# Where the large buffers and weight tiles begin in a partition: a two-layer hybrid trunk on one core

## The chip, the cores and the metric

One core of a Trainium2 chip. The metric is the device time of one launch in microseconds (us). The kernel before takes 2214.97 us, the median of three runs (2214.35 to 2215.24).

## The reference

The input is 256 tokens of 2048 float32 channels. Layer 0 is a hybrid mixer: an RMSNorm, one input projection (2048 to 11296 columns), a Mamba-2 state-space group of 32 heads and a stick-breaking attention group of 16 heads, and one output projection from the 4096 joined channels. Layer 1 is a pooling mixer with trailing means of 2, 4, 8 and 16 tokens and a linear map of 512 by 512 for each of its four groups. Each layer ends in an MLP with a squared ReLU. In the reference's words:

```python
def sq_relu_mlp(h, w_up, w_down):
    u = jax.nn.relu(h @ w_up)
    return (u * u) @ w_down

for layer in range(DEPTH):
    ...
    x = x + mix.astype(x.dtype)
    x = x + sq_relu_mlp(rms_norm(x, mlp_norm[layer]), mlp_w_up[layer], mlp_w_down[layer]).astype(x.dtype)
```

With a hidden width of 8192 the two MLPs hold most of the multiplications; every weight is read from HBM once.

## The kernel before

All products with weights form one stream. `plan()` lists it as units (a block of output columns) and steps (what one DMA of 512 KB brings: two k-tiles of 512 columns, or four of 256). For each step SP loads the weights into a `raw` tile, ScalarE copies them to a `hi` tile (line 182) and VectorE puts the rest into a `lo` tile (line 183); `feed` keeps loads six steps and splits three steps ahead of TensorE. The activations lie in the same form, a high and a low part, in fourteen large buffers that `slot(i)` hands out (`st0` to `st13`, 8192 bytes in each partition: high or low part, four k-tiles, 256 tokens). A product is made of three: high by high, low by high, high by low, all in the type float32r. Small work (norms, the state-space scan, attention, pooling) is cut into generators that `tick` advances between steps, so that its TensorE instructions stand between those of the stream.

There are two orders of a product, and in each TensorE reads two things from SBUF: the moving operand that it streams now, and the stationary weights of the next product, which it loads meanwhile.

- Not turned (line 820: the projections to B, z, q, k, v, the output projection, `down`, `pool`): the activations in `st` are stationary, 128 by 128; the weights in `hi` or `lo` move, 512 columns (256 in the last two units, 288 in one). Three products for each k-tile and half of the tokens.
- Turned (lines 812 and 814: `c1`, the eight `x` units and all `up` units): 128 columns of `hi` or `lo` are stationary ("weights that stay"), and the activations in `st` move: line 812 streams both parts of a k-tile (2 by 256 columns) against `hi`, line 814 the high part (256 columns) against `lo`. One of each is a pair here; a unit has 32 pairs.

**Where tiles begin.** A tile pool gives each tag its place in a partition when the tag is first used, one behind the other, each rounded up to 32 bytes. Before the pool lie a scratch area of 16384 bytes for dynamic DMAs and 128 bytes of constants. The first places are `cst` (2560 bytes), `prm` (808), `row` (384), `mhalf` (32) and three `ev` tiles; then the large tags follow in the order in which the stream first needs them, with small ones between. So the built kernel before has these starting addresses modulo 256 (in bytes, the same in each partition):

| tiles | start modulo 256 | what they hold |
|---|---|---|
| `hi`, `lo` (4 of each, 4096 bytes) | 96 | split weights |
| `st0`, `st1`, `st2`, `st3` | 96 | normed input of layer 0's projection and `up`; hidden of layer 1's blocks 0, 2 |
| `st8`, `st9` | 96 | merged heads; hidden of layer 0's blocks 1, 3; normed input of layer 1's `up` |
| `st10`, `st11` | 192 | the same as `st8`, `st9` |
| `st4`, `st7` | 128 | merged heads; hidden of layer 0's blocks 0, 2 and of layer 1's blocks 1, 3 |
| `st5`, `st6` | 64 | the same as `st4`, `st7` |

Within these tiles every operand begins a multiple of 512 bytes from the start (of 128 in the one unit of 288 columns). Below, the **distance** of a product is the start of the weights loaded during it minus the start of what it streams, modulo 256.

The MLPs run as blocks: eight `up` units (256 turned pairs), then four `down` units (384 products of 512 columns), four such blocks for each layer. Where the hidden values of a block lie is set by `gen_u`'s `base`, `((4, 8), (0, 4))[layer][b % 2]`.

Of the kernel before, what the change touches and what calls it, by code (L numbers as in the profile page):

```python
# [11 lines left out]
F32R = mybir.dt.float32r  # L12
# [4 lines left out]
P = 128  # L17
# [7 lines left out]
NB = DFF // FB  # L25
WINS = (2, 4, 8, 16)

# columns of the input projection: z | x | B | C | dt | q | k | v
CZ, CX, CB, CC = 0, 2048, 4096, 4608
CQ, CK, CV = 5152, 7200, 9248  # L30

# per-partition parameters (channel = tile * 128 + partition)
P_HYB, P_MLP, P_POOL, P_CW, P_CB, P_ON, P_QN, P_KN = 0, 16, 48, 64, 160, 184, 200, 201
NPRM = 202

# constant matrices
K_ID, K_U, K_SL, K_ONE, K_LT = 0, 128, 256, 384, 512
NCST = 640

# where in the weight stream (unit, k-tile) the quarters of x for the first norm are loaded  # L40
X_EARLY = ((0, 14), (1, 2), (1, 6), (1, 10))
AHEAD_LOAD = 6
WARM = 2
AHEAD_SPLIT = 3


def plan():
    """The products with weights in their order. A unit is a block of output columns; a step is
    the part of its weights that one DMA brings: [128, k-tiles, columns]."""
    units = []  # L50

    def unit(w, r0, nk, c0, n, kind, arg, src, k0=0, turned=False):
        units.append(dict(w=w, r0=r0, nk=nk, c0=c0, n=n, kind=kind, arg=arg, src=src, k0=k0,
                          turned=turned))

    unit("w_in", 0, KT, CB, 512, "b", None, "h")
    unit("w_in", 0, KT, CC + 256, 288, "c2", None, "h")
    unit("w_in", 0, KT, CC, 256, "c1", None, "h", turned=True)
    for g in range(4):
        for h in range(2):  # L60
            unit("w_in", 0, KT, CX + 512 * g + 256 * h, 256, "x", (g, h), "h", turned=True)
        unit("w_in", 0, KT, CZ + 512 * g, 512, "z", g, "h")
    for j in range(4):
        unit("w_in", 0, KT, CK + 512 * j, 512, "k", j, "h")
        unit("w_in", 0, KT, CQ + 512 * j, 512, "q", j, "h")
        unit("w_in", 0, KT, CV + 512 * j, 512, "v", j, "h")
    for c in range(4):
        unit("w_out", 0, 2 * KT, 512 * c, 512, "out", c, "merged")
    for layer in range(2):
        if layer == 1:  # L70
            for g in range(4):
                unit("pool_w", 512 * g, 4, 0, 512, "pool", g, "pool", 4 * g)
        for b in range(NB):
            for i in range(8):
                unit("w_up", D * layer, KT, b * FB + 256 * i, 256, "up", (layer, b, i),
                     f"mlp{layer}", turned=True)
            for c in range(4):
                n = 256 if (layer, b, c) == (1, NB - 1, 3) else 512
                for c0 in range(512 * c, 512 * c + 512, n):
                    unit("w_down", DFF * layer + b * FB, KT, c0, n, "down", (layer, b, c), "u")  # L80

    steps, off = [], 0
    for u, d in enumerate(units):
        ks = list(range(0, d["nk"], 4 if d["turned"] else 2))
        if u == 0:
            ks = [0, 1, 2, 3] + ks[2:]
        for k, e in zip(ks, ks[1:] + [d["nk"]]):
            steps.append((u, k, e - k, off))
            off += (e - k) * P * d["n"]
    return units, steps  # L90
# [3 lines left out]
def tile_trunk(ctx: ExitStack, tc: tile.TileContext, x_in, xt_in, w_all, prm_in,  # L94
# [27 lines left out]
    def v3(ap, a, b):  # L122
        return ap.rearrange("p (a b) -> p a b", a=a, b=b)

    # ------------------------------------------------------------ constants
    x_sb = []
    cst = new("cst", [P, NCST])
    prm = new("prm", [P, NPRM])
# [7 lines left out]
        return prm[:, i : i + 1]  # L136

    def load_x(q):
        """half of the tokens' rows, half of the columns at a time"""
        m, c = q // 2, slice(D // 2 * (q % 2), D // 2 * (q % 2) + D // 2)  # L140
        if q == 0:
            x_sb[:] = [slot(12 + m, (P, D), F32) for m in range(MT)]
        nc.sync.dma_start(x_sb[m][:, c], x_in[m * P : m * P + P, c])

    # ------------------------------------------------------------ the weight stream
    hT, merged = {}, {}
    u_blk, pT, hM = {}, {}, [{}, {}]
    sources = {"h": hT, "merged": merged, "pool": pT, "mlp0": hM[0], "mlp1": hM[1], "u": u_blk}
# [21 lines left out]
    def split(i):  # L170
        u, k, nk, _ = steps[i]
        n = units[u]["n"]
        raw = raws.pop(i)
        if u == 0:
            for kk in range(k, k + nk):
                if kk % 4 == 0:
                    hx.append(slot(kk // 4))
                put_hi_lo(hx[-1], kk % 4, xt[kk // 8][:, kk % 8], pcol(P_HYB + kk))
                hT[kk] = (hx[-1], kk % 4)
        hi, lo = (v3(new(tag, [P, 1024], F32R, bufs=4)[:, : nk * n], nk, n)  # L180
                  for tag in ("hi", "lo"))
        act.activation(hi, raw, AF.Copy)  # L182
        dve.tensor_tensor(lo, raw, hi.bitcast(F32), ALU.subtract)  # L183
        splits[i] = hi, lo
# [6 lines left out]
            split(done["split"])  # L191
            done["split"] += 1

    # ------------------------------------------------------------ work beside the weight stream
    lane, lane2 = deque(), deque()
    flags = set()

# [14 lines left out]
            assert lane or lane2  # L212
            tick()

    # ------------------------------------------------------------ norms
    def power(dst, src, mean):
        """dst = (src * mean + eps) ** -0.5"""
        n = src.shape[-1]
        t = new("pw", [P, 8], bufs=2)[:, :n]
        dve.tensor_scalar(t, src, mean, EPS, ALU.mult, ALU.add)  # L220
        pool.tensor_tensor(dst, t, mhalf[:, :n], ALU.pow)  # L221

    def put_hi_lo(dst, c, ps, gain=None):
        """dst[:, 0/1, c] = the high and low parts of ps (times a per-partition gain)"""
        if gain is None:
            act.activation(dst[:, 0, c], ps, AF.Copy)  # L226
            dve.tensor_tensor(dst[:, 1, c], ps, dst[:, 0, c].bitcast(F32), ALU.subtract)  # L227
        else:
            act.activation(dst[:, 0, c], ps, AF.Copy, scale=gain)  # L229
            dve.scalar_tensor_tensor(dst[:, 1, c], ps, gain, dst[:, 0, c].bitcast(F32),  # L230
                                     ALU.mult, ALU.subtract)

    def to_ring(src, tiles, kt0, dst, gain):
        """src[m]: [128 tokens, 512]; four k-tiles of 256 tokens into dst and tiles[kt0...]"""
        for h in range(2):
            b = bank()
            bv = v3(b, 2, T)
            for c in range(2):
                for m in range(MT):
                    k = 2 * h + c  # L240
                    pe.transpose(bv[:, c, m * P : (m + 1) * P],  # L241
                                 src(m)[:, k * P : (k + 1) * P], ident)
            if gain is None:
                put_hi_lo(dst, slice(2 * h, 2 * h + 2), bv)
            else:
                for c in range(2):
                    put_hi_lo(dst, 2 * h + c, bv[:, c], pcol(gain + kt0 + 2 * h + c))
            for c in range(2):
                k = 2 * h + c
                tiles[kt0 + k] = (dst, k)  # L250
            yield
# [1 line left out]
    rs = {}  # L253

    def spread(name):
        """rs[name, "row"][p, t] = rs[name] of token t, for all p"""
        r = rs[name]
        dg = v3(t4(2 * P), MT, P)
        for m in range(MT):
# [7 lines left out]
        rs[name, "row"] = o  # L267

    def add_halves(dst, ps):
        """dst = the sum of the two halves of each bank"""  # L270
        act.activation(dst, ps[:, :, T:], AF.Copy)  # L271
        dve.tensor_tensor(dst, ps[:, :, :T], dst, ALU.add)  # L272

# [21 lines left out]
        if c == 3 and name != "pool":  # L295
            yield from spread(name)

    # ------------------------------------------------------------ SSD
    ssd = {}

    def evac(ps, n, r):
# [3 lines left out]
        return e  # L305

    def turn(e, n):
        """e: [tokens, n * 128 channels] -> [channel, n, 3 + 256 tokens]"""
        yield
        yield  # L310
        xT = v3(t4(n * 259), n, 259)
# [14 lines left out]
        return xT  # L326

    def conv(xT, ct0, n, dst):
        """xT: [channel, n, 3 + 256 tokens] -> dst [channel, n, 256 tokens] = silu(conv + b)"""
        dve.memset(xT[:, :, 0:3], 0.0)  # L330
        for c in range(n):
            w = P_CW + 4 * (ct0 + c)
# [7 lines left out]
                yield  # L340

    def gen_dt(pre):
        """pre: [128, 64] dt before softplus, (chunk, head)"""
        e, t, q, da = (ssd["tmp"][:, 1792 + 64 * i : 1856 + 64 * i] for i in range(4))
        # log1p(e) = 2 artanh(e / (2 + e)), e = exp(-|pre|) in (0, 1]
        act.activation(e, pre, AF.Abs)
        act.activation(e, e, AF.Exp, scale=-1.0)
        dve.tensor_scalar(t, e, 2.0, None, ALU.add)
# [153 lines left out]
        dst = slot(8 + g)  # L502
        yield from to_ring(lambda m: y[:, m], merged, 4 * g, dst, P_ON)

    # ------------------------------------------------------------ stick-breaking attention
    at = {}

    def gen_qk(kind, j, e):
# [113 lines left out]
                merged[16 + 4 * j + 2 * i + h] = (dst, 2 * i + h)  # L622
            yield

    # ------------------------------------------------------------ MLP and pooling
    def gen_u(i, ea, eb, base):
        yield
        act.activation(eb, ea, AF.Square)  # L628
# [117 lines left out]
            dve.scalar_tensor_tensor(ea, ea, 0.0, row2(name), ALU.max, ALU.mult)  # L746
            lane.append(gen_u(i, ea, eb, ((4, 8), (0, 4))[layer][b % 2]))

    # ------------------------------------------------------------ the stream
    act.dma_start(prm, prm_in)  # L750
    act.preload_act_table_set("silu_and_others")
    mhalf = new("mhalf", [P, 8])
    pool.memset(mhalf, -0.5)
    # keeps the tensor engine's clock up until the first weights are there
    wt = new("ev", [P, MT, 512], bufs=3)
    dve.memset(wt[:, 0], 0.0)
    wb = bank()
# [3 lines left out]
    hx, late = [], []  # L761

    def startup():
        """the first norm's scale and small constants"""
        ss = new("ss", [P, MT, 4], bufs=2)
        for q in range(4):
            m, h = q // 2, q % 2
# [20 lines left out]
    i = 0  # L788
# [103 lines left out]
```

## Time and profile before

| | |
|---|---|
| median of three runs | 2214.97 us |
| span of the profiled execution | 2214.3 us |
| TensorE busy | 2207.0 us in 11045 instructions |
| weight loads beside it | 1854.0 us |
| VectorE, ScalarE, GpSimd busy | 1325.4, 1113.0, 21.7 us |
| read from HBM | 412.57 MB, 187 GB/s over the span |

The page gives no time for the profiled execution beyond its span; the span lies 0.7 us under the median. "Busy" of TensorE counts a modelled end, and the spans of neighbours overlap, so the mean duration of a matmul (389 ns) is longer than the time from one start to the next. Where TensorE never idles, that time (the pitch) is the busy time of a window divided by the products in it; a window's count also holds one to three products that reach over its edges, so the products are counted here from the code.

### The profile page before, as it was taken

The numbers are of one execution on the slowest core, as the hardware profiler recorded it, in microseconds if no ns is written. First come the engines' busy times: TensorE is split into PE (matmuls) and PEld (weight loads), VectorE is DVE, ScalarE is ACT, GpSimd is POOL, SyncE is SP. The second block draws the span as 40 slices with busy tenths as digits, with TensorE's granted clock in tenths as the row PEclk, the third lists the DMA queues.
The fourth block names the chain that finished last, engine by engine and source line by source line (L and its number), as shares of the span: only waits on it lengthen the run. The fifth ranks groups of instructions, "written<-read, shape, count | busy, mean of one in ns | idle before, by whom it ended". The sixth has DMA issues, their size and how long they took to land.

```text
span 2214.3 us, 28392 instructions
## 1 busy us (share of the span) xinstructions
PE 2207.0 (100%) x11045; PEld 1854.0 (84%) x11045; DVE 1325.4 (60%) x1554; ACT 1113.0 (50%) x1325; POOL 21.7 (1%) x21
## 2 busy tenths in 40 slices
PE   9999999999999999999999999999999999999999
PEld 7888888888888888888888888888888888888888
DVE  6988756655645565555555466577555645655654
ACT  7665456665544454354344345456534534544543
POOL 0000000000000000000000000000000000000000
PEclk9999999999999999999999999999999999999999
DMA  8654555555665566556566666555666656565564
GB/s 300 213 196 162 163 184 167 163 179 170 202 187 184 181 186 186 189 186 189 187 189 190 204 219 190 181 171 163 190 196 187 188 189 190 187 193 191 190 195 148
DMA packets 118630, 416.56 MB, mean 188 GB/s; under 512 B 13344, under 2 KB 16096, under 8 KB 118240
## 3 DMA queue, kind: packets, MB, share of 16 engines
q1 hardware_dynamic: 117632, 413.60, 59.0%
q8 instruction: 86, 1.41, 0.3%
q10 hardware_dynamic: 864, 1.15, 0.2%
q14 instruction: 48, 0.39, 0.1%
HBM read 412.57 MB, written 2.13 MB: 187 GB/s over the span
## 4 chain that ended last, share of the span: by engine, by line
PE 99%; DMA 0%; DVE 0%; ACT 0%; issue 0%; SPq 0%; DVEq 0%; ACTq 0%
PE acc L820 58%; PE acc L812 25%; PE acc L814 13%; PE bg L469 1%; PE bg L241 1%; DMA raw<-w_all 0%; PE bg L526 0%; PE bg L616 0%; PE bg L561 0%; PE bg L437 0%; PE bg L557 0%; PE bg L618 0%; PE bg L474 0%; PE bg L480 0%; DVE lo L183 0%; PE bg L577 0%
## 5 line engine op out<-in xcount | busy, mean ns | idle before, releaser
L183 DVE TENSOR_TENSOR lo<-raw,hi 128x1024 fp32r<-128x1024 f32 (+2 forms) x774 | 931.4, 1205 | 777.5 <-ACT hi L182 762.9
L182 ACT ACTIVATE hi<-raw 128x1024 fp32r<-128x1024 f32 (+2 forms) x774 | 808.5, 1045 | 1033.8 <-PE acc L820 642.7
L820 PE MATMUL acc<-hi,st 128*128 128x512 f32 (+2 forms) x3840 | 1175.2, 389 | 1.4 <-ACT hi L182 1.4
L820 PEld LDWEIGHTS acc<-hi,st 128*128 128x128 f32 x3840 | 709.9, 188 | 153.4 <-ACT hi L182 3.5
L812 PE MATMUL acc<-st,hi 128*128 128x512 f32 x2336 | 826.1, 398 | 0.0
L820 PE MATMUL acc<-lo,st 128*128 128x512 f32 (+2 forms) x1920 | 740.7, 387 | 0.1
L814 PE MATMUL acc<-st,lo 128*128 128x256 f32 x2336 | 654.8, 280 | 0.0
L812 PEld LDWEIGHTS acc<-st,hi 128*128 128x128 f32 x2336 | 438.3, 188 | 106.1 <-issue 1.4
L814 PEld LDWEIGHTS acc<-st,lo 128*128 128x128 f32 x2336 | 440.5, 189 | 2.0 <-issue 1.2
L820 PEld LDWEIGHTS acc<-lo,st 128*128 128x128 f32 x1920 | 360.4, 188 | 78.1 <-DVE lo L183 0.5
L706 DVE TENSOR_TENSOR st<-st,acc 128x512 f32<-128x512 f32 (+1 forms) x74 | 46.5, 669 | 29.1 <-PE acc L820 29.1
L746 DVE SCALAR_TENSOR_TENSOR ev<-ev,rrow 128x512 f32<-128x512 f32 x64 | 44.3, 692 | 2.2
L227 DVE TENSOR_TENSOR st<-ev,st 128x512 fp32r<-128x512 f32 x64 | 44.3, 692 | 0.2
L272 DVE TENSOR_TENSOR ev<-acc,ev 128x512 f32<-128x512 f32 x64 | 43.7, 683 | 0.0
L226 ACT ACTIVATE st<-ev 128x512 fp32r<-128x512 f32 x64 | 40.6, 634 | 2.0
L229 ACT ACTIVATE st<-bg,prm 128x256 fp32r<-128x256 f32 x64 | 28.4, 468 | 24.9 <-DVE st L230 22.8
L628 ACT ACTIVATE ev<-ev 128x512 f32<-128x512 f32 x64 | 39.5, 617 | 0.0
L271 ACT ACTIVATE ev<-acc 128x512 f32<-128x512 f32 x64 | 37.2, 582 | 0.0
L230 DVE SCALAR_TENSOR_TENSOR st<-bg,prm,st 128x256 fp32r<-128x256 f32 x64 | 29.4, 478 | 6.0 <-ACT st L229 6.0
L336 DVE SCALAR_TENSOR_TENSOR t<-t,prm,t 128x256 f32<-128x256 f32 x48 | 19.6, 476 | 0.0
L221 POOL TENSOR_TENSOR qrs<-pw,mhalf 128x8 f32<-128x8 f32 x8 | 15.6, 1952 | 246.4 <-DVE pw L220 246.4
L516 DVE TENSOR_TENSOR ev<-ev,qrs 128x1024 f32<-128x1024 f32 x8 | 9.8, 1225 | 13.5 <-POOL qrs L221 13.5
(155 smaller groups left out, 595.7 us busy)
## 6 DMA issues: line engine op xcount, KB each, us to landing
raw<-w_all SPq DMA_DIRECT2D x746, 512.0 KB, 3.5
raw<-w_all SPq DMA_DIRECT2D x20, 256.0 KB, 3.1
st<-x_in SPq DMA_DIRECT2D x8, 512.0 KB, 5.3
st<-scr SPq DMA_DIRECT2D x8, 512.0 KB, 5.8
raw<-w_all SPq DMA_DIRECT2D x8, 288.0 KB, 4.5
st<-prow_in SPq DMA_DIRECT2D x2, 1024.0 KB, 5.3
st<-xt_in SPq DMA_DIRECT2D x6, 256.0 KB, 6.3
st<-pmat_in SPq DMA_DIRECT2D x1, 768.0 KB, 5.1
```

The source lines that it names most:

```text
L182: act.activation(hi, raw, AF.Copy)
L183: dve.tensor_tensor(lo, raw, hi.bitcast(F32), ALU.subtract)
L226: act.activation(dst[:, 0, c], ps, AF.Copy)
L227: dve.tensor_tensor(dst[:, 1, c], ps, dst[:, 0, c].bitcast(F32), ALU.subtract)
L271: act.activation(dst, ps[:, :, T:], AF.Copy)
L272: dve.tensor_tensor(dst, ps[:, :, :T], dst, ALU.add)
L628: act.activation(eb, ea, AF.Square)
L706: dve.tensor_tensor(x_sb[m][:, cs], x_sb[m][:, cs], ps[:, m, : d["n"]], ALU.add)
L746: dve.scalar_tensor_tensor(ea, ea, 0.0, row2(name), ALU.max, ALU.mult)
L812: pe.matmul(ps[:, f].rearrange("p (h t) -> p h t", h=2), hi[:, kk, fs], t[:, :, c], start=first, stop=False)
L814: pe.matmul(ps[:, f, :T], lo[:, kk, fs], t[:, 0, c], start=False, stop=last)
L820: pe.matmul(ps[:, m, :n], t[:, h % 2, c, m * P : (m + 1) * P], (hi, hi, lo)[h][:, kk], start=first and h == 0, stop=last and h == 2)
```

## The change

The constants of the module get `PAD, TURN = 24, 56`. Ahead of all other tiles the kernel takes a tile `pad` of 24 floats, then one tile of each of the fourteen `slot`s, then four tiles each of `hi` and `lo`, none of which is used; this fixes the places of these tags. `hi` and `lo` grow from 1024 to 1088 floats, 4352 bytes, which is 17 times 256. A turned unit uses its tile from float 56 on, which is 224 bytes; all others from float 0. The scratch area for dynamic DMAs shrinks from 16384 to 1024 bytes. Comments go. No instruction is added, removed or moved.

```diff
+PAD, TURN = 24, 56
 ...
+    new("pad", [P, PAD])
+    for i in range(14):
+        slot(i)
+    for tag in ("hi", "lo"):
+        for _ in range(4):
+            new(tag, [P, 1088], F32R, bufs=4)
 ...
-        hi, lo = (v3(new(tag, [P, 1024], F32R, bufs=4)[:, : nk * n], nk, n)
+        o = TURN if units[u]["turned"] else 0
+        hi, lo = (v3(new(tag, [P, 1088], F32R, bufs=4)[:, o : o + nk * n], nk, n)
                   for tag in ("hi", "lo"))
 ...
-    nc = _bacc.Bacc("TRN2", target_bir_lowering=False, num_devices=1)
+    nc = _bacc.Bacc("TRN2", target_bir_lowering=False, num_devices=1,
+                    dynamic_dma_scratch_size=1024)
```

## The prediction

> **What bounds the kernel now.** I read the page's busy times first, then the chain that ended last, then the busy time by stage, then TensorE's timeline inside a stage. The page:
>
> ```profile
> span 2214.3 us, 28392 instructions
> PE 2207.0 (100%) x11045; PEld 1854.0 (84%) x11045; DVE 1325.4 (60%) x1554; ACT 1113.0 (50%) x1325; POOL 21.7 (1%) x21
> ...
> PEclk9999999999999999999999999999999999999999
> ...
> PE acc L820 58%; PE acc L812 25%; PE acc L814 13%; PE bg L469 1%; PE bg L241 1%; DMA raw<-w_all 0%; PE bg L526 0%; PE bg L616 0%; PE bg L561 0%; PE bg L437 0%; PE bg L557 0%; PE bg L618 0%; PE bg L474 0%; PE bg L480 0%; DVE lo L183 0%; PE bg L577 0%
> ```
>
> TensorE is never without work (2207.0 of 2214.3 us), its granted clock is full in all slices, and 96% of the chain is lines 820, 812 and 814. So the time is a number of products times the pitch from one start to the next, and only a change of the pitch counts. The feed is ahead, as the view of waits shows: ScalarE's split waits for TensorE to free a `hi` tile, while TensorE's weight loads waited for a split for 3.5 us in the whole span.
>
> ```profile
> engine line waited for: us in total, times, longest us
> ...
> ACT hi L182 <- PE acc L820: 642.7, 414, 4.1
> ...
> PEld acc L820 <- ACT hi L182: 3.5, 4, 1.3
> ```
>
> Now the view of busy time by stretch, for stretches that begin and end with whole units or runs of k-tiles (us, then busy time and count of TensorE, weight loads, VectorE, ScalarE, GpSimd, then clock and DMA):
>
> ```profile
> core 0: us, PE busy (x) PEld busy (x) DVE busy (x) ACT busy (x) POOL busy (x), PEclk, DMA share, GB/s
> 834.17:923.74 89.57, 89.57 (x387) 72.05 (x385) 44.80 (x41) 35.64 (x36) 0.00 (x0) 1.00 0.60 188
> 1587.93:1675.01 87.08, 87.08 (x387) 72.07 (x385) 44.80 (x41) 35.71 (x36) 0.00 (x0) 1.00 0.62 193
> 1014.18:1102.71 88.53, 88.53 (x386) 72.19 (x385) 44.79 (x41) 35.75 (x36) 0.00 (x0) 1.00 0.62 190
> 1193.16:1282.74 89.58, 89.58 (x386) 72.05 (x385) 46.88 (x45) 35.62 (x36) 0.00 (x0) 1.00 0.66 213
> 1373.19:1464.52 91.33, 91.33 (x411) 74.53 (x409) 53.49 (x59) 44.68 (x59) 0.00 (x0) 1.00 0.58 184
> 1764.65:1854.22 89.57, 89.57 (x386) 72.05 (x385) 44.80 (x41) 35.62 (x36) 0.00 (x0) 1.00 0.60 188
> 2120.59:2187.77 67.18, 67.18 (x291) 54.04 (x289) 32.19 (x31) 25.87 (x28) 0.00 (x0) 1.00 0.59 181
> 2187.77:2210.33 22.56, 22.56 (x193) 22.52 (x191) 10.86 (x17) 8.20 (x13) 0.00 (x0) 1.00 0.48 149
> 2142.98:2148.58 5.60, 5.60 (x26) 4.51 (x24) 3.65 (x4) 2.09 (x2) 0.00 (x0) 1.00 0.85 259
> 2148.58:2159.78 11.20, 11.20 (x49) 9.00 (x48) 4.90 (x4) 4.27 (x5) 0.00 (x0) 1.00 0.61 198
> 2190.61:2196.21 5.60, 5.60 (x50) 5.60 (x49) 2.75 (x5) 2.54 (x4) 0.00 (x0) 1.00 0.71 210
> ```
>
> The first two are the key: both are four `down` units of 384 equal products (line 820, 512 columns), with the same DMA load and other work. In the first the hidden values lie in `st4` to `st7` (distances 32 and 224, from the table of places) and a product takes 89.57 / 384 = 233.3 ns; in the second they lie in `st0` to `st3` (distance 0), 87.08 / 384 = 226.8 ns. The third, half at 0 and half at 96, stands between: 230.5. Within one unit at distances 32 and 224, the ninth row has 24 products at 32 (233.3 ns each) and the tenth 48 at 224 (233.3). So a distance of 0 is worth 6.5 ns of each such product. The eleventh row is 48 products of 256 columns at 224: 116.7 ns.
>
> **The part that I can read off: products that are not turned.** By the same rule of places the kernel after starts its pool at 1024 + 128 = 1152; `pad` takes 96 bytes, so `st0` begins at 1248, which is 224 modulo 256. All fourteen `st` are 8192 bytes and all `hi` and `lo` 4352, both multiples of 256: all begin at 224. So every product of line 820 gets distance 0, and 226.8 ns (in the unit of 288 columns the k-tiles alternate between 0 and 128, as now: nothing). By stretch, against 87.08:
>
> - layer 0's `down`: blocks 0 and 2, 89.57 and 89.58: -2.49 and -2.50; blocks 1 and 3, half of them off distance: -1.45 each (the second, 91.33, also holds norms, which stay);
> - layer 1's `down`: block 1, 89.57: -2.49; block 3, the 288 products of 512 columns: 67.18 against 288 x 0.2268 = 65.3, -1.9; its last 192 products of 256 columns (22.56 us, 117.5 ns each) have no row at distance 0; half of a product of 512 at distance 0 would be 113.4 ns, so the gain lies between 0 and -0.8, and I take -0.3;
> - the output projection: 24 of its 32 k-tiles lie off distance (`st4` to `st7`, `st10`, `st11`), so 4 x 144 products x 6.5 ns: -3.7;
> - q, k, v, z, B and `pool` are at 0 already: nothing.
>
> Sum: -16.3 us.
>
> **The part that I can't: turned pairs.** Here the activations move from 224 and the weights are loaded from 224 + 224 = 448, 192 modulo 256: distance 224 for all 2336 pairs (c1 and x 9 units, `up` 64, 32 pairs each). Now they stand at 0, or, for half of layer 1, at 160 (`st10`, `st11`). Two stretches of eight `up` units, layer 0 and layer 1, and the halves of one of layer 1's units:
>
> ```profile
> 923.74:1014.18 90.44, 90.44 (x513) 78.41 (x512) 54.02 (x55) 45.37 (x53) 0.00 (x0) 1.00 0.59 187
> 1675.01:1764.65 89.64, 89.64 (x514) 78.41 (x512) 54.02 (x55) 45.40 (x53) 0.00 (x0) 1.00 0.61 188
> 1531.93:1537.49 5.56, 5.56 (x35) 4.90 (x34) 4.12 (x5) 3.76 (x5) 0.00 (x0) 1.00 0.60 189
> 1537.49:1543.13 5.64, 5.64 (x35) 4.90 (x33) 2.73 (x3) 2.12 (x2) 0.00 (x0) 1.00 0.68 189
> ```
>
> A pair takes 353.3 ns in layer 0 (90.44 / 256) and 350.2 in layer 1; in the halves 347.5 (distance 0) and 352.5 (160). So distance 0 alone does not fix a pair: layer 0 and that first half have the same distance. The timeline shows two steady patterns (start, then duration):
>
> ```profile
> 924.08 0.40 PE L812 MATMUL acc<-st,hi 128*128 128x512 f32 x1
> 924.32 0.28 PE L814 MATMUL acc<-st,lo 128*128 128x256 f32 x1
> 924.43 0.40 PE L812 MATMUL acc<-st,hi 128*128 128x512 f32 x1
> 924.67 0.28 PE L814 MATMUL acc<-st,lo 128*128 128x256 f32 x1
> 924.79 0.40 PE L812 MATMUL acc<-st,hi 128*128 128x512 f32 x1
> 925.03 0.28 PE L814 MATMUL acc<-st,lo 128*128 128x256 f32 x1
> 925.14 0.40 PE L812 MATMUL acc<-st,hi 128*128 128x512 f32 x1
> ...
> 1533.67 0.39 PE L812 MATMUL acc<-st,hi 128*128 128x512 f32 x1
> ...
> 1534.71 0.39 PE L812 MATMUL acc<-st,hi 128*128 128x512 f32 x1
> ```
>
> In layer 0 three unequal pairs repeat: 0.35, 0.36, 0.35, together 1.06 us, 353.3 each. In layer 1 three pairs take 1534.71 - 1533.67 = 1.04 us, 346.7 each. No pair stands at 224 in this trace. The bounds: from below 226.8 + 113.4 = 340.2, the best product of 512 and half of it; from above the slowest pair of the three, 924.43 to 924.79, about 361. The nearest rows are those at 224 in line 820: 233.3 + 116.7 = 350.0. Against them speaks that all steady pairs fall into a few patterns, the best at 346.7. I take the middle of the two, 348.3. Per 256 pairs that is 89.17:
>
> - layer 0's `up`: 90.44 to 89.17, -1.27, four times: -5.1;
> - layer 1's `up`: 89.64 to 89.17, -0.47, four times: -1.9;
> - c1 and x, 288 pairs among other work that hides which pattern they have: between 346.7 and 353.3, so 0 within 1 us.
>
> Sum: -7.0 us. With the bounds: at 340.2, -13.4 - 10.2 - 2.9 = -26.5; at 361, +7.9 + 11.1 + 3.2 = +22.2.
>
> **What costs nothing.** The unused tiles issue nothing, and no order on any queue changes. The DMAs are as many, and land in `raw` at another place; a load of 512 KB lands in 3.5 us, and six are ahead:
>
> ```profile
> raw<-w_all SPq DMA_DIRECT2D x746, 512.0 KB, 3.5
> ```
>
> If that cover went, a step of line 820 (12 products, 2.7 us) would have to wait for a load; TensorE would gain gaps. The scratch area serves a queue that this kernel doesn't use for data: weights come by SP's. About 610 other products (transposes, scan, attention) get new places too; at some ns each, 2 us either way.
>
> **Sum.** 2214.97 - 16.3 - 7.0 = 2191.7 us. The profiled execution (2214.3) is 0.7 us under the median, so its terms carry over.
>
> **Rivals.**
>
> - *Nothing happens: 2215 us.* The difference between the two `down` stretches would come from something that goes with the buffers, not with their start. For it: distance and buffer change together in all rows. Against it: the stretch on `st8` to `st11`, of which half begin like `hi`, stands halfway (230.5 ns). The Trainium skill ("SBUF — State Buffer", section "SBUF: two separate sides") says that TensorE has two independent read ports for the moving operand and the weights and never waits on anyone; by that rule where the operands begin would not matter, and this rival would be the outcome. The rows (233.3 against 226.8 ns) disagree with it. Chance 0.06.
> - *The turned pairs gain nothing:* 224 keeps them between 350.5 and 354, as 160 does (352.5). That is -2.4 to +5.8 us instead of -7.0: 2196 to 2204 us. For it: line 820 is slower at 224 than at 0. Chance 0.22.
> - *The turned pairs fall to a pattern that this trace doesn't have,* 340 to 345 ns: 2172 to 2183 us. For it: the best products of line 820 and half of one add up to that; against it, no steady pattern of the trace is that fast. Chance 0.16.
> - *The turned pairs get slower:* weights loaded 32 bytes behind the stream collide with it in lines 812 and 814, and the streams of line 814, half as long, are stalled as often. At 361 ns everywhere the time is 2214.97 - 16.3 + 22.2 = 2220.9. It is slower than before from 16.3 / 2336 = 7.0 ns above today's mean of about 351.5, at 358.5. For it: the slow third pair is a collision of this kind. Chance 0.06, half of it on the slow side.
>
> **How the numbers follow.** My forecast (pairs at 345 to 350.5) has 0.50 and its own range is 2183 to 2196. From 2174 to 2205 about 0.82 lies: below stay the deepest cases of the third rival, above the first and last. A measurement here tells 0.2% (4.4 us) from no change. Faster: 0.50 + 0.22 + 0.16 = 0.88; the first rival and the milder half of the last give 0.08 for the same, and 0.04 is slower.
>
> **What would show it.** Stretches of four `down` units at 87.1 us in both layers, whatever block; a stretch of the output projection about 0.94 us shorter for each unit; eight `up` units near 89.2, the same in layer 0 and layer 1, with one steady pattern. Unchanged DMA rows and waits of TensorE. Wrong it would be if `down` at distance 0 kept 89.57 in blocks 0 and 2 (then the start is not the cause), or if `up` stretches passed 91.8 (358.5 ns).

## The result and the profile after

The changed kernel takes 2189.57 us (median of four runs, 2188.69 to 2189.96), against 2215.10 us for the kernel before beside it: a ratio of 0.9884, 95% interval 0.987 to 0.9898. The forecast was 2191.7 us, 2174 to 2205.

First the page, then the view of busy time by stretch (start and end in us, then length, and busy time and count of TensorE, weight loads, VectorE, ScalarE, GpSimd, the clock and DMA), for the stretches that answer to those shown of before. Lines 812, 814 and 820 of before are 823, 825 and 831 here.

```profile
span 2187.9 us, 28392 instructions
...
PE 2180.8 (100%) x11045; PEld 1857.1 (85%) x11045; DVE 1325.4 (61%) x1554; ACT 1115.1 (51%) x1325; POOL 21.7 (1%) x21
```

```profile
core 0: us, PE busy (x) PEld busy (x) DVE busy (x) ACT busy (x) POOL busy (x), PEclk, DMA share, GB/s
555.20:737.94 182.74, 182.74 (x825) 151.42 (x823) 98.35 (x102) 87.53 (x106) 0.00 (x0) 1.00 0.62 195
828.29:915.35 87.06, 87.06 (x387) 72.08 (x386) 44.77 (x41) 35.84 (x36) 0.00 (x0) 1.00 0.62 193
915.35:1004.10 88.75, 88.75 (x514) 78.67 (x513) 54.05 (x55) 45.41 (x53) 0.00 (x0) 1.00 0.61 190
1004.10:1091.15 87.05, 87.05 (x386) 72.07 (x385) 44.77 (x41) 35.84 (x36) 0.00 (x0) 1.00 0.62 193
1179.90:1266.96 87.06, 87.06 (x387) 72.08 (x385) 46.70 (x45) 35.84 (x36) 0.00 (x0) 1.00 0.68 218
1355.71:1445.66 89.95, 89.95 (x411) 74.42 (x410) 53.48 (x59) 44.64 (x59) 0.00 (x0) 1.00 0.59 187
1655.28:1744.03 88.75, 88.75 (x514) 78.67 (x512) 54.05 (x55) 45.41 (x53) 0.00 (x0) 1.00 0.62 190
1744.03:1831.08 87.05, 87.05 (x386) 72.07 (x385) 44.77 (x41) 35.84 (x36) 0.00 (x0) 1.00 0.61 193
2095.64:2160.93 65.29, 65.29 (x291) 54.06 (x289) 32.18 (x31) 26.04 (x28) 0.00 (x0) 1.00 0.61 187
2160.93:2183.96 23.03, 23.03 (x193) 22.98 (x191) 10.86 (x17) 8.20 (x13) 0.00 (x0) 1.00 0.49 144
```

The first row is the output projection with what runs beside it; before, it was

```profile
555.81:742.21 186.40, 186.40 (x824) 151.50 (x823) 98.33 (x102) 87.27 (x106) 0.00 (x0) 1.00 0.60 191
```

The instructions, the busy time of VectorE and the clock are as before; TensorE is still almost never idle, and does the same products in 26 us less. Stretches of four `down` units (87.05 and 87.06) no longer depend on the block. Eight `up` units take 88.75 us in both layers, 346.7 ns for a pair. The timeline of layer 0's `up` (start, duration) shows one pattern, three pairs in 916.74 - 915.70 = 1.04 us:

```profile
915.70 0.39 PE L823 MATMUL acc<-st,hi 128*128 128x512 f32 x1
915.92 0.28 PE L825 MATMUL acc<-st,lo 128*128 128x256 f32 x1
916.04 0.39 PE L823 MATMUL acc<-st,hi 128*128 128x512 f32 x1
...
916.74 0.39 PE L823 MATMUL acc<-st,hi 128*128 128x512 f32 x1
```

### The profile page after: what moved, and what is told of

The parts are those of the page before. It is cut to its first block, busy times and chain, and to the rows that moved or that the text cites. A ratio compares the mean times of both kernels' runs of the same rounds, so it can differ in the third digit from the quotient of the medians.

```text
span 2187.9 us, 28392 instructions
## 1 busy us (share of the span) xinstructions
PE 2180.8 (100%) x11045; PEld 1857.1 (85%) x11045; DVE 1325.4 (61%) x1554; ACT 1115.1 (51%) x1325; POOL 21.7 (1%) x21
## 4 chain that ended last, share of the span: by engine, by line
PE 98%; DMA 1%; DVE 0%; ACT 0%; SPq 0%; issue 0%; POOL 0%; DVEq 0%; ACTq 0%; POOLq 0%
PE acc L831 57%; PE acc L823 24%; PE acc L825 13%; PE bg L480 1%; PE bg L252 1%; DMA raw<-w_all 0%; DMA st<-x_in 0%; PE bg L537 0%; PE bg L627 0%; PE bg L572 0%; DVE lo L194 0%; PE bg L448 0%; PE bg L568 0%; PE bg L629 0%; PE bg L491 0%; PE bg L485 0%
## 5 line engine op out<-in xcount | busy, mean ns | idle before, releaser
L823 PE MATMUL acc<-st,hi 128*128 128x512 f32 x2336 | 815.4, 392 | 0.0
```

The source lines that it names most:

```text
L823: pe.matmul(ps[:, f].rearrange("p (h t) -> p h t", h=2), hi[:, kk, fs], t[:, :, c], start=first, stop=False)
```

## The experiments

Each starts from the kernel after. "Distance" is as above: start of the weights that a product loads for the next one, minus start of what it streams, modulo 256. e3 (2209.62 us), e5 (2212.20), e6 (2198.78), e7, e8 (2191.69) and e10 (2242.98) are one launch each; they are read by the pitch inside the trace, not by their time. In blocks with other work beside the stream a pitch is read from the difference to the same stretch of the kernel after.

**e1: without the offset of the weights that stay.**

```diff
-PAD, TURN = 24, 56
+PAD, TURN = 24, 0
```

> The change without its second part: TURN is 0, so all large tiles begin at 224 modulo 256 and every product, turned ones too, has distance 0. Theory (the distance sets the pitch): the four down units of a block stay at 87.07 us as in the kernel after; the turned pairs fall into the two patterns that distance 0 had before, 353.3 ns in layer 0 and 346.7 ns in layer 1, so the stretches of eight up units are 90.4 and 88.8 us, and the time is 2189.6 + 1024 x 6.67 ns = 2196.4 us; 2190 to 2203 if the patterns fall otherwise. Rival (the offset of the weights that stay does nothing, the new places did it all): 2189.6 us and 88.8 us in all stretches of up.

Measured: 2201.17 us (2200.26 to 2202.79), ratio 0.994 (0.9925 to 0.9954). By stretch: `down` of layer 0's block 0, `up` of layer 0's block 2, of layer 1's block 1 and, in the last two rows, of block 0 of layer 1 and of layer 0:

```profile
828.44:915.49 87.05, 87.05 (x386) 72.08 (x385) 44.77 (x41) 35.84 (x36) 0.00 (x0) 1.00 0.59 193
1093.00:1183.44 90.44, 90.44 (x514) 78.41 (x512) 54.05 (x55) 45.51 (x53) 0.00 (x0) 1.00 0.59 186
1660.72:1751.16 90.44, 90.44 (x514) 78.39 (x512) 54.05 (x55) 45.52 (x53) 0.00 (x0) 1.00 0.58 186
1478.77:1573.64 94.87, 94.30 (x548) 82.29 (x547) 64.71 (x81) 54.05 (x79) 0.70 (x1) 1.00 0.56 175
737.93:828.44 90.51, 90.51 (x525) 79.05 (x524) 56.43 (x64) 48.39 (x61) 0.70 (x1) 1.00 0.59 186
```

`down` has its whole gain without the offset; six of the eight stretches of `up` have none: 353.3 ns, now in layer 1 too. The exceptions are the last two rows: with other work in them, they are within 0.2 us of what they are in the kernel after (94.75 and 90.35), so their pairs ran at about 347 ns at the same distance and with the same buffers as the stretches of their layer above them. A distance can hold two patterns. What decides between them is not shown: both exceptions have small work between their pairs, but so has layer 0's first stretch of `up` in the kernel before, which took 91.96 us at distance 0. Layer 1 as a whole did not stay in the fast pattern, as I had expected.

**e2: the offset alone.** The tiles that are taken ahead go, so every tag has the start modulo 256 that it had before.

```diff
-    new("pad", [P, PAD])
-    for i in range(14):
-        slot(i)
-    for tag in ("hi", "lo"):
-        for _ in range(4):
-            new(tag, [P, 1088], F32R, bufs=4)
```

> The change without its first part: no tile is taken ahead, so all tags have the starts modulo 256 of the kernel before (hi and lo at 96, st at 96, 128, 64 or 192), and turned weights begin 224 bytes into their tile: distance 224 where the activations start at 96, 128 where they start at 192. Theory: down stays at 89.57, 88.5 and 87.08 us by block as before; up in layer 0 falls from 90.44 to 88.8 us, in layer 1 to between 88.8 and 89.7; time 2215 - 6.8 - 1 to 3 = 2205 to 2207 us. Rival (the new places did it all): 2215 us.

Measured: 2207.51 us (2207.07 to 2207.79), ratio 0.9967 (0.9954 to 0.998). `down` and `up` of layer 0, `up` of layer 1:

```profile
832.26:921.83 89.57, 89.57 (x386) 72.06 (x385) 44.80 (x41) 35.62 (x36) 0.00 (x0) 1.00 0.59 188
921.83:1010.58 88.75, 88.75 (x513) 78.67 (x512) 54.03 (x55) 45.37 (x53) 0.00 (x0) 1.00 0.59 190
1667.68:1757.01 89.33, 89.33 (x513) 78.67 (x512) 54.00 (x55) 45.36 (x53) 0.00 (x0) 1.00 0.59 189
```

The mirror of e1: `up` has its gain, `down` stays at 89.57. In layer 1 half of the pairs get distance 128 instead of 224, and 0.58 us of each stretch is missing. That is why the parts do not quite add up: by spans e1 saves 15.8 us and e2 8.3, together 24.1 of 26.4, and layer 1's four stretches of some 0.57 us are the missing 2.3. (What `up` changes in e1, 2.1 us gained in the two exceptions and 2.4 us lost in layer 1's other three, cancels but for 0.3 us.)

**e3: a map of distances.** Block n of the eight MLP blocks gets an offset of 32n bytes, in `up` and in `down`.

```diff
-        o = TURN if units[u]["turned"] else 0
+        o = offset(units[u])   # up, down: 8 * (4 * layer + block) floats
```

> The kernel after, but in block n of the eight MLP blocks the weights of up and of down begin 32 x n bytes into their tiles: n = 0 to 3 in layer 0, 4 to 7 in layer 1. One run maps distance 32n for turned pairs and -32n for products that are not turned. Theory: the pitch follows the distance alone. Not turned: 226.7 ns in block 0 only, 233.3 in blocks 1 (distance 224) and 7 (distance 32), 234 in block 5 (distance 96), the others between 226 and 236. Turned: 346.7 per pair in block 7 (224), 346.7 or 353.3 in block 0, about 351 in block 5 (160), the others between 340 and 361. Rival (the buffers or their order matter, not the start): 226.7 and 346.7 ns in all blocks, 2189.6 us.

Rows of `down` at offsets 32, 64, 128, 160 and 192 bytes, then of `up` at 32 (64 is the same), 96, 160 and 192 (224 takes 88.76 us, as in the kernel after):

```profile
1004.95:1094.54 89.59, 89.59 (x386) 71.98 (x385) 44.80 (x41) 35.64 (x36) 0.00 (x0) 1.00 0.59 188
1184.99:1272.89 87.90, 87.90 (x386) 72.12 (x385) 46.75 (x45) 35.69 (x36) 0.00 (x0) 1.00 0.66 217
1577.46:1666.69 89.23, 89.23 (x386) 72.35 (x385) 44.77 (x41) 35.66 (x36) 0.00 (x0) 1.00 0.60 189
1756.30:1846.27 89.97, 89.97 (x387) 72.32 (x385) 44.76 (x41) 35.66 (x36) 0.00 (x0) 1.00 0.59 187
1935.59:2025.17 89.58, 89.58 (x386) 72.19 (x385) 44.75 (x41) 35.71 (x36) 0.00 (x0) 1.00 0.58 188
914.51:1004.95 90.44, 90.44 (x514) 78.54 (x512) 54.03 (x55) 45.35 (x53) 0.00 (x0) 1.00 0.58 187
1272.89:1361.64 88.75, 88.75 (x513) 78.11 (x512) 54.24 (x56) 46.78 (x54) 0.00 (x0) 1.00 0.61 197
1666.69:1756.30 89.61, 89.61 (x513) 78.17 (x512) 54.02 (x55) 45.41 (x53) 0.00 (x0) 1.00 0.57 188
1846.27:1935.59 89.32, 89.32 (x514) 78.22 (x513) 54.03 (x55) 45.40 (x53) 0.00 (x0) 1.00 0.59 189
```

Divided by 384 products and 256 pairs:

| distance (bytes) | 32 | 64 | 96 | 128 | 160 | 192 | 224 | 0 (after, e1) |
|---|---|---|---|---|---|---|---|---|
| `down`, ns | 233.3 | 233.3 | 234.3 | 232.4 | about 233 | 228.9 | 233.3 | 226.7 |
| `up`, ns for a pair | 353.3 | 353.3 | 346.7 | about 351 | 350.0 | 348.9 | 346.7 | 353.3 or about 347 |

(32 in `down` is the 288 products of the last block, 67.20 us. Two stretches hold other work and are read from their difference to the kernel after: 160 in `down`, 92.22 against 89.95 us, and 128 in `up`, 95.76 against 94.75.) The same buffers, the same order, and the pitch follows the start: the rival that it goes with the buffers falls. The two orders of a product have different best distances.

**e4: another start for all.**

```diff
-PAD, TURN = 24, 56
+PAD, TURN = 32, 56
```

> The kernel after with a pad of 128 instead of 96 bytes: all large tiles begin at 0 modulo 256 instead of 224, and all distances stay. Theory (only the distance counts): 2189.6 us, same within 0.1%, down at 87.07 and up at 88.8 us. Rival (the start itself counts, 0 being a multiple of 64 and 224 not): pitches change in both, down by some ns per product (more than 1 us per stretch).

Measured: 2189.00 us (2188.61 to 2191.13), ratio 0.9886 (0.987 to 0.9903), and the same stretches:

```profile
827.83:914.88 87.05, 87.05 (x386) 72.07 (x385) 44.76 (x41) 35.83 (x36) 0.00 (x0) 1.00 0.62 193
914.88:1003.63 88.75, 88.75 (x513) 78.67 (x512) 54.04 (x55) 45.42 (x53) 0.00 (x0) 1.00 0.60 190
```

Of these two starts neither is better; of what was tried, the distance counts and not the common start. The kernel before, with yet other starts, had 233.3 ns at 32 and at 224 as e3 has.

**e5: a finer map.** As e3, with offsets of 4, 8, 16, 24, 48, 80, 112 and 256 bytes.

> The kernel after, but the weights of up and of down begin 4, 8, 16 and 24 bytes into their tiles in the blocks of layer 0, and 48, 80, 112 and 256 bytes in those of layer 1. Theory (the pitch follows the distance modulo 256, in pieces of 32 bytes): the last block behaves as distance 0, products that are not turned 226.7 ns; within the first 32 bytes they stay near 226.7 ns, and the other three have what the nearest multiples of 32 gave in the map, 228.9 to 234.3 ns. Rival 1 (only equal starts are fast, any other offset collides): 233 ns in all blocks but the last. Rival 2 (it is not modulo 256, the tile's distance in whole counts): the last block at 228 to 234 ns.

`down` at offsets of 4, 8, 16 and 112 bytes, and the 288 products at 256:

```profile
828.62:919.49 90.87, 90.87 (x386) 72.04 (x385) 44.83 (x41) 35.79 (x36) 0.00 (x0) 1.00 0.60 185
1008.81:1098.40 89.59, 89.59 (x386) 72.41 (x385) 44.80 (x41) 35.84 (x36) 0.00 (x0) 1.00 0.59 188
1187.16:1276.13 88.97, 88.97 (x387) 72.21 (x385) 46.87 (x45) 35.79 (x36) 0.00 (x0) 1.00 0.65 214
1938.91:2027.65 88.74, 88.74 (x387) 71.97 (x385) 44.80 (x41) 35.68 (x36) 0.00 (x0) 1.00 0.60 190
2118.09:2183.39 65.30, 65.30 (x290) 54.08 (x289) 32.19 (x31) 26.02 (x28) 0.00 (x0) 1.00 0.61 186
```

At 256 bytes it is 65.30 / 288 = 226.7 ns again: modulo 256 holds (rival 2 falls). But four bytes are enough to lose it: 236.6 ns, more than any multiple of 32, then 233.3 at 8, 231.7 at 16, 231.1 at 112. My theory of pieces of 32 bytes falls; for `down` rival 1 is nearer, though not with one value. `up` at 16, 24 and 48 bytes comes out at 88.76 and 88.77 us or, in the stretch with the norms, at the 94.75 us of the kernel after: no distance tried that both parts share brings a pair under 346.7 ns.

**e6: shorter loads.** In `down` fewer columns of the stationary activations are loaded in 14 of 16 k-tiles.

```diff
+                w = (112, 96, 80, 72)[d["arg"][1]]   # down, inner k-tiles; else P
-                    pe.matmul(ps[:, m, :n], t[:, h % 2, c, m * P : (m + 1) * P],
+                    pe.matmul(ps[:w, m, :n], t[:, h % 2, c, m * P : m * P + w],
```

> The kernel after, but in the down units all k-tiles but the first and the last load only 112, 96, 80 and 72 of the 128 columns of the stationary activations, by block, and so leave out the products of the other tokens; in layer 1 the moving weights begin 32 bytes into their tile (distance 224). What streams stays 512 columns. Theory (the time above 512 columns is the load of the next weights colliding with the stream, once for each piece that is loaded): at distance 0 a product costs 213.3 + 13.3 x columns / 128, so 225.0, 223.3, 221.7 and 220.8 ns in layer 0, and at distance 224 213.3 + 20 x columns / 128, so 230.8, 228.3, 225.8 and 224.6 ns. Rival (a fixed cost of changing weights, 13.3 ns, with collisions only in the 6.7 ns that the distance adds): 226.7 ns in all blocks of layer 0; in layer 1 226.7 plus a part of 6.7 ns. 213.3 ns is 512 times the 106.7 ns by which products of 512 and 256 columns at distance 0 differ (226.7 and 120.0), divided by 256.

The stretches with 112, 96 and 80 columns of layer 0 (distance 0), and the same of layer 1 (224):

```profile
827.52:915.32 87.80, 87.80 (x386) 67.59 (x385) 44.78 (x41) 35.77 (x36) 0.00 (x0) 1.00 0.62 192
1004.07:1092.33 88.26, 88.26 (x387) 63.20 (x385) 44.80 (x41) 35.76 (x36) 0.00 (x0) 1.00 0.60 191
1181.08:1270.40 89.32, 89.32 (x386) 58.73 (x385) 46.87 (x45) 35.81 (x36) 0.00 (x0) 1.00 0.66 214
1572.98:1661.17 88.19, 88.19 (x386) 67.38 (x385) 44.81 (x41) 35.66 (x36) 0.00 (x0) 1.00 0.62 191
1749.94:1837.31 87.37, 87.37 (x387) 63.10 (x385) 44.81 (x41) 35.67 (x36) 0.00 (x0) 1.00 0.60 193
1926.06:2014.89 88.83, 88.83 (x387) 58.57 (x386) 44.79 (x41) 35.63 (x36) 0.00 (x0) 1.00 0.60 189
```

The loads are shorter (weight loads busy 72.08 us in the kernel after, here 67.59, 63.20, 58.73). At distance 0 the products got slower all the same: with the 48 whole ones at 226.7, the short ones take (87.80 - 10.88) / 336 = 228.9, then 230.3 and 233.5 ns. At 224 they got faster, 229.1, 226.7 and 231.0 instead of 233.3, in no order of their length; 72 columns come out at about 230.7 ns at distance 0 and 231.1 at 224. A shorter load also makes the product write fewer rows of its sum; the two are not separated here. Both the theory (a price for each piece loaded) and the rival (a fixed price at distance 0) fall.

**e7: streams of 256 columns.** The `down` units are cut in two, but in the last block of layer 0.

```diff
-                n = 256 if (layer, b, c) == (1, NB - 1, 3) else 512
+                n = 512 if (layer, b) == (0, NB - 1) else 256
+            return (8, 16, 24, 0, 32, 40, 48, 56)[4 * d["arg"][0] + d["arg"][1]]   # floats, down
```

> The kernel after with the down units cut in two of 256 columns each (but in the last block of layer 0), and their moving weights 32, 64 and 96 bytes into the tile in blocks 0 to 2 of layer 0, and 128, 160, 192 and 224 bytes in layer 1: distances 224, 192, 160 and 128, 96, 64, 32 for streams of 256 columns. Distance 0 took 120.0 ns in the kernel after, 224 took 116.7 and 32 took 118.4 in the kernel before. Theory (a stream no longer than the load is stalled less at other distances than one of 512 columns): all seven lie under 120.0 ns, and 224 and 32 come out at 116.7 and 118.4 again, whatever the buffer. Rival (distance 0 is best for any stream, and the last units of the kernel after are slower for another reason): the seven lie at 120.0 ns or more. The time is longer than that of the kernel after by about 2300 more products x 7 to 13 ns, so 2205 to 2225 us.

The time was 2210.73 us. 384 products at distance 224, 192 and 160:

```profile
828.67:873.48 44.81, 44.81 (x387) 44.81 (x385) 25.83 (x41) 21.72 (x35) 0.00 (x0) 1.00 0.66 184
1007.03:1050.55 43.52, 43.52 (x386) 43.52 (x385) 25.84 (x41) 21.66 (x35) 0.00 (x0) 1.00 0.67 188
1182.84:1228.92 46.08, 46.08 (x386) 46.08 (x385) 25.98 (x41) 21.68 (x35) 0.00 (x0) 1.00 0.59 179
```

116.7, 113.3 and 120.0 ns; the others, from 128 down to 32, lie between 117.3 and 118.7. So 224 and 32 repeat what the kernel before had in other buffers, and a stream of 256 columns is best at 192, not at 0: it has a map of its own. (At 160 it is no better than at 0, against the theory's "all seven under 120.0".)

**e8 and e9: a start for each part.** Line 823 (512 columns) covers the load of `lo`, line 825 (256 columns) that of `hi`; so by the maps `lo` should stand at distance 0 and `hi` at 192. e8 tries eight pairs of offsets by block, e9 takes the best everywhere and moves the last two units to 192.

```diff
-                  for tag in ("hi", "lo"))
+                  for tag, o in zip(("hi", "lo"), starts(units[u])))
+    def starts(d):      # e9, in floats
+        if d["turned"]:
+            return 48, 0
+        return (16, 16) if d["n"] == 256 else (0, 0)
```

> The kernel after, but in the up units the hi and the lo part of the weights that stay begin at different places in their tiles. During line 823 (512 columns stream) the lo part is loaded, during line 825 (256 columns) the hi part. Offsets of (hi, lo) in bytes by block: layer 0 (192, 0), (224, 0), (96, 0), (0, 192); layer 1 (192, 64), (208, 0), (176, 0), (160, 0). Theory (each product's pitch goes by the distance of the load that it covers and by its own length, as the two maps have them: 512 columns 226.7 ns at 0, 228.9 at 192, 233.3 at 64; 256 columns 113.3 at 192, 116.7 at 224, 117.3 at 96, 120.0 at 0 and 160): pairs of 340.0, 343.4, 344.0 and 348.9 ns in layer 0, so stretches of 87.0 (block 0 holds other work beside it, 1.6 us more), 87.9, 88.1 and 89.3 us; block 0 of layer 1, 346.6, block 3 346.7, the two between them are not in the map. Rival (346.7 ns is the floor of a pair, since distances 16, 24, 48, 96 and 224 all come out there): no stretch under 88.75 us.

> The kernel after with the hi part of the weights that stay 192 bytes into its tile and the lo part 0 bytes, and with the last two units, whose streams have 256 columns, at distance 192 (64 bytes into their tiles). Theory (each product by its own load and length): pairs of 340.0 instead of 346.7 ns, 2336 x 6.67 = 15.6 us less; the last 192 products 113.3 instead of 120.0 ns, 1.3 us less; 2189.6 - 16.9 = 2172.7 us. Rival (346.7 is the floor of a pair): 2188.3 us. Slower than the kernel after if the pairs fall into a slow pattern, as at distance 0 (353.3 ns): 2204 us.

e8, `up` with (hi, lo) at (224, 0) and (208, 0):

```profile
913.23:1001.40 88.17, 88.17 (x513) 78.17 (x512) 54.08 (x55) 45.38 (x53) 0.00 (x0) 1.00 0.61 191
1653.56:1744.01 90.45, 90.45 (x514) 78.93 (x512) 54.04 (x55) 45.38 (x53) 0.00 (x0) 1.00 0.58 187
```

e9, eight `up` units of layer 0, and the last products of 256 columns:

```profile
911.76:998.81 87.05, 87.05 (x513) 77.24 (x512) 54.10 (x55) 45.48 (x53) 0.00 (x0) 1.00 0.63 194
2145.73:2168.35 22.62, 22.62 (x193) 22.57 (x191) 10.85 (x17) 8.18 (x13) 0.00 (x0) 1.00 0.52 149
```

e9 takes 2174.48 us (2174.06 to 2176.54), ratio 0.9819 (0.9806 to 0.9833) to the kernel before, 15 us under the kernel after: 87.05 / 256 = 340.0 ns for a pair, at the lower bound of the prediction, reached with two distances where none of one did. The time is 2 us above the 2172.7 expected. In e8 (192, 0), beside other work, gave 88.70 us (88.6 expected), (192, 64) in layer 1 about 346.8 ns (346.6 expected) and (224, 0) 88.17 us (344.4 ns, 343.4 expected); (96, 0), (0, 192) and (160, 0) lay 1 to 3 ns above what the maps add up to; (176, 0) and (208, 0), of which the maps have nothing, came out at 351.6 and 353.3. (0, 192) took 350.0 ns, its mirror (192, 0) in e9 340.0: what counts is the weights being loaded; if it were those in use, the two would come out the other way round. So the theory of each product's own load led to the best version and is right to about 3 ns for these pairs. It is no rule, though: for the common distances of e3 the same sum gives 228.9 + 113.3 = 342.2 ns at 192, where 348.9 was measured, and 234.3 + 117.3 = 351.6 at 96, where it was 346.7. The last products, at 117.8 ns instead of 113.3, again show two patterns for one distance.

**e10: length of the load, length of the stream.** As e6 with 64, 32, 120 and 104 columns; in the last two blocks of layer 1 whole loads and units of 384 and 128 columns.

> The kernel after with other lengths of load and stream in the down units. In layer 0 and in blocks 0 and 1 of layer 1 all k-tiles but the first and last load only 64, 32, 120 and 104 columns of the stationary activations, by block (64 and 32 in layer 1), and leave out the products of the other tokens; layer 0 is at distance 0, these two blocks of layer 1 at 224. Blocks 2 and 3 of layer 1 load all 128 columns at distance 0 and are cut in units of 384 and 128 columns. Theory (what a load leaves behind for the next repeats when its length is a multiple of 256 bytes): 64 columns, 256 bytes, run at 226.7 ns at distance 0 like 128, while 32, 120 and 104 columns lie above it, at 228 to 233. Rival (a load of fewer columns always costs more at distance 0, whatever its length): 64 columns lie above 228 ns too. For the stream: if the floor is a part of every column (226.7 / 512 = 113.3 / 256 = 0.443 ns), 384 columns take 170.0 ns; if it is a sum for each product (13.3 ns over 0.417 ns per column), 173.3 ns.

64 columns at distance 0, then one unit of 384 columns and one of 128 (96 products each):

```profile
828.49:916.66 88.17, 88.17 (x386) 54.09 (x385) 44.84 (x41) 35.76 (x36) 0.00 (x0) 1.00 0.61 191
1957.51:1974.21 16.70, 16.70 (x98) 16.70 (x98) 7.04 (x11) 5.51 (x8) 0.00 (x0) 1.00 0.41 130
1946.84:1957.51 10.67, 10.67 (x98) 10.67 (x97) 5.34 (x10) 4.64 (x8) 0.00 (x0) 1.00 0.65 190
```

With 64 columns a short product takes (88.17 - 10.88) / 336 = 230.0 ns: the theory falls, the rival holds; at distance 0 every shorter load tried costs more (32 columns 232.2 ns, 120 233.4, 104 about 228.7). At 224, 64 and 32 columns take 230.9 and 233.1. 384 columns of stream take 174.0 ns. From 256 to 512 columns a product at distance 0 costs 0.417 ns per column and some 13.3 ns besides (120.0, 174.0, 226.7 for 256, 384, 512). Below, this sum fails: 128 columns take 10.67 / 96 = 111.1 ns, where it gives 66.7. There the weight loads lie one behind the other without a gap (busy 10.67 of 10.67 us), so they may be the limit; that is not shown. If they are, the best pitch of 256 columns (113.3 ns) is close to that limit too.

## Why the prediction held, step by step

- **Products that are not turned** (forecast -16.3 us): blocks 0 and 2 of layer 0 went from 89.57 and 89.58 to 87.06, block 1 from 88.53 to 87.05, block 3 from 91.33 to 89.95, layer 1's block 1 from 89.57 to 87.05 and the 288 products from 67.18 to 65.29: -12.3 against -12.3 forecast. The output projection, 186.40 us before and now 182.74, gave -3.7, as forecast. Distances taken from the tags' order were enough.
- **The one wrong sign:** the last 192 products, forecast -0.3, came out +0.5 (22.56 to 23.03). The step that failed is the price of a stream of 256 columns at distance 0 as half of one of 512. From 256 to 512 columns the 13.3 ns of e10 come once for each product and do not shrink with its columns: 120.0 ns, not 113.4.
- **Turned pairs** (forecast 348.3 ns, -7.0 us): 346.7 in all stretches, layer 0 from 90.44 to 88.75, layer 1 from 89.64 to 88.75; the four stretches of each give -6.7 and -3.5, -10.2 in all. The term was sized 3.2 us short: of the two numbers whose middle I took, the best pattern already in the trace was right, and the sum of two rows of line 820 (350.0) was not. Lines 823 and 825 at 224 do not take 233.3 and 116.7 ns: by the starts in the trace, over the stretch from 915.35, they take 228.4 and 118.3 on average. `c1` and `x`, forecast at 0 within 1 us, gave -0.6.
- **What costs nothing:** VectorE's busy time is the same (1325.4 us), ScalarE's 2 us more. One wait of TensorE appeared in the profiled execution, near 39 us, for a `lo` split: the unit of 288 columns, forecast at nothing, took 13.32 us instead of 12.74. Its other products kept their pitch, and in e4 it takes 12.74 again, so the wait does not come from the distances.
- **The rivals.** *Nothing happens* falls with e3: one and the same stretch takes 87.05 or 89.59 us by where the moving operand starts. The rule of the Trainium skill ("SBUF — State Buffer", section "SBUF: two separate sides") that TensorE's two read ports are independent, from which this rival followed, does not foretell these 226.7 and 233.3 ns. *The turned pairs gain nothing* was the state at distance 0 (e1) and not at 224. *A pattern that this trace doesn't have* exists, 340.0 ns, but not for a common offset: e9 needed two. *The turned pairs get slower*: no distance of e3 reached the 358.5 ns from which it would decide; the slowest was 353.3.

The forecast change of -23.3 us came out 2.2 us short in medians (25.5) and 3.1 in spans (26.4). The turned pairs gave 3.2 us more than forecast and `c1` and `x` 0.6; the last products missed by 0.8 the other way, and that these partly cancel is luck. The chances of "same" and "slower" do not follow from the rivals either: 0.06 and half of 0.06 make 0.09 and leave 0.03, not 0.08 and 0.04.

The profiled execution of before does not lie under the median. A span is 1.8 us shorter than its launch (2187.9 of 2189.73 after), so the span of 2214.3 belongs to about 2216.1 us, 1 us above the median. That is why spans fell by more than medians.

**What stays open.** That the pitch goes with the distance between the weights being loaded and the stream is shown by e1 to e5 and used by e9. That the two reads get in each other's way is the nearest reading, but no run shows it, or how. Two reads that meet in the same place would fit a period of 256 bytes, but four bytes of offset doing the most harm, and shorter loads making distance 0 slower, do not follow from any simple picture that I tried. Nor is it shown where the 13.3 ns at distance 0 go, what decides between two patterns at one distance, or why the two maps add up for some pairs and not for others.

## What to carry to other kernels

Where TensorE is never idle, divide a stretch's length by its products and compare stretches of equal products: a difference in pitch with equal clock and DMA load is worth asking after the addresses. Give the operands of a hot loop explicit places (large tiles first, sizes a multiple of 256 bytes) so that the distance between what is loaded and what streams is the same everywhere, then map a few offsets in one run, a block each, for each length of stream. A price read for one length of stream should not be scaled to another.

## What the runs showed of the hardware that was not expected

- The pitch of a float32r product depends on the distance between the stationary operand being loaded and the moving one in SBUF, modulo 256 bytes and down to 4 bytes: 226.7 to 236.6 ns for 512 columns, 113.3 to 120.0 for 256, 340.0 to 353.3 for a pair; two common starts made no difference (2189.00 and 2189.57 us).
- A shorter weight load at distance 0 makes the product slower (228.9 ns with 112 columns, 233.5 with 80, against 226.7 with 128).
- One distance can hold two steady patterns (353.3 and about 347 ns for a pair at 0 in e1, 113.3 and 117.8 ns for 256 columns at 192 in e7 and e9).
- A stream of 128 columns at distance 0, with a load of 128 columns for each product, is hardly cheaper than one of 256: 111.1 against 120.0 ns.
